# Attention scores laid out by query half, two plain groups of heads where there were four, and a normalisation whose rows go through memory

## The chip, the cores and the metric

The kernel runs on one core of a Trainium2 chip. The metric is the device time of one execution in microseconds (us). Three runs of the kernel before took 2332.04, 2332.18 and 2333.17 us, so its time is the median, 2332.18 us. The engines are called PE (matmuls; PEld loads its weights), DVE (vector work), ACT (scalar work, copies and casts), POOL (here mostly the issue of stores) and SP (the issue of loads).

## The reference

One step of a four-layer decoder over 1024 prompt tokens and 8 single-token samples, width 2048, all in float32. Layers "A" mix by pooling, layers "B" by attention within a window of 128 over keys and values that are projected once. The kernel computes one layer of each kind:

```
A:  z = x @ w_in_a                 # 2048 -> 4096: a branch u and a gate
    y = (group_linear(pool(u) - u) * scale * silu(gate)) @ w_out_a
    h = layer_norm(ALPHA * x + y)
kv: k, v = h @ w_kv                # 4 heads of 64, k rotated
B:  z = h @ w_in_b                 # 2048 -> 4096: 32 query heads of 64, and a gate
    s = q . k / 8 within the window of 128, else -1e30
    m = max(max_k s, sink)         # a learned sink for each head
    p = exp(s - m) / (sum_k exp(s - m) + exp(sink - m))
    y = ((p @ v) * silu(gate)) @ w_out_b
    out = layer_norm(ALPHA * h + y)
```

Outputs are the rows of both paths and the new states of pool, keys and values.

## The kernel before

**Products.** A float32 product is made of three matmuls in a rounded float32 type: high parts with high, high with low, low with high. So every 128x1024 tile of weights that arrives is first cast by ACT (L488, the high part), then DVE subtracts the cast from the tile (L503, the low part, here called the prep). A weight tile then feeds 24 matmuls; that is called a run here, and runs are numbered from the program's start.

**Two ways to multiply.** Tokens are cut into chunk 0 (512 prompt tokens) and chunk 1 (512 and the 8 samples). Most phases multiply by a Strassen-Winograd scheme (the method `seven`, L658 to L660): a pair of weight rows (four blocks) takes seven runs of 24 matmuls over half the tokens (256 or 260 columns). It needs sums of weight blocks (DVE adds, L293 or L346) and sums of the activations, made by `t_ops` (DVE, L826 to L829) and stored by POOL (L830) to the tiles tx, tg, th, to. Two phases are plain (the method `unit`, L686 to L688): four weight tiles per pair, 48 matmuls of 512 columns for each 128 rows of output. The phases run in the order ai (A's input product), ao (its output product), bi (B's input product with the attention in it), bo, each for both chunks; `PHASES` lists them, `PLAIN` names the plain ones. In bi the unit of work is a group p of 0 to 7: a pair of w_in_b for queries and one for gates, four heads of attention.

**Attention.** For each pair of heads (t, two per group) `attend` has the PE write scores into a bank S of PSUM (L1761), ACT copy one part of them into a memory tile (L1778), DVE put the other part in where the mask says so (`copy_predicated`, L1782, 128x1024 elements) and reduce to maxima (L1787); ACT takes the exponentials (L1798) and scales them (L1820), PE transposes (L1825), ACT copies out (L1833), DVE masks a part (L1834), PE multiplies with the values (L1863), DVE gates (L1891) and POOL stores the result (L1894, tile o).

**Order and memory.** ACT, DVE and PE each execute their instructions in the order in which the program issues them; nothing overtakes. Before each run `begin` loads weights for up to 7 runs ahead, casts up to 4 and preps up to 3 ahead (5, 4, 3 where plain). After each run `end` emits due events and, every so many runs (`every`) and if enough tiles are free (`room`), one step of a side job, such as the layer norm `ln_gen`. All of it lives in 54 tiles of on-chip memory (128x1040 floats, named m0 to m53; a trace shows them as m). A new tile is put where a tile was freed longest ago; one freed behind a store counts as freed 10 releases later (`Mem.full`, `Slot.free`). Before anything is written into such a place, its last reader, a store too, must be done.

**The norm between the layers.** `ln_gen` for chunk 1 runs as a side job in the plain bi phase: it subtracts the mean (L962), squares (L965), multiplies by the reciprocal deviation (L1000), scales and shifts (L991), stores h and calls `t_ops` for th1. The eight tiles stay on chip from the subtraction to the end.

Of the kernel before, what the change touches and what calls it, by code (L numbers as in the profile page):

```python
# [11 lines left out]
U8 = mybir.dt.uint8  # L12
# [4 lines left out]
P = 128  # L17
# [7 lines left out]
NH = 32  # L25
# [4 lines left out]
NEG = -1e30  # L30
TP = 512
NB = TP // P
# [18 lines left out]
    ("ai", 0, (0, 1)), ("ai", 0, (1, 4)), ("ai", 1, (0, 4)), ("ao", 0, None), ("ao", 1, None), ("bi", 0, (0, 4)),  # L51
    ("bi", 0, (4, 8)), ("bi", 1, (0, 8)), ("bo", 0, None), ("bo", 1, None),
# [129 lines left out]
class Kern:  # L182
    def __init__(self, ctx, tc, io):
# [12 lines left out]
        self.mki = one.tile([P, 2, P], U8, name="mki")  # L196
# [37 lines left out]
    def use_four(self, wide):  # L234
# [97 lines left out]
    def first_pair(self, name, q):  # L332
# [8 lines left out]
        def add(out, x, y, i):  # L341
            def go():
# [4 lines left out]
                self.nc.gpsimd.dma_start(ws[:, i, :], s[out].a[:, :1024])  # L347
# [3 lines left out]
        def free(*ks):  # L351
            return [lambda k=k: s.pop(k).free(k != "c") for k in ks]
# [20 lines left out]
    def build_stream(self):  # L373
        io = self.io
        w = []
        for kind, c, part in PHASES:
# [535 lines left out]
    def ln_gen(self, c, pre, acc, gc, bc, out, td):  # L912
# [39 lines left out]
        w = self.mem.full()  # L952
        q, v = w.a[:, :T], w.a[:, TMAX : TMAX + T]
        if c == 0:
            nc.vector.tensor_mul(q, mu, mu)
        else:
            sq, sqs = self.mem.full(), {}
            for p in range(10):
# [4 lines left out]
                if 1 <= p <= 8:  # L963
                    sqs[p - 1] = sq if p == 1 else self.mem.full()
                    nc.scalar.activation(flat(sqs[p - 1]), flat(pre[p - 1]), AF.Square)  # L965
                yield
# [5 lines left out]
            for go in self.j_steps(T, s2[:, 0], s2[:, 1], var, sq):  # L972
                go()
                yield
# [1404 lines left out]
```

## Time and profile before

| | us |
|---|---|
| median of three runs | 2332.18 |
| the profiled execution | 2332.49 |
| its span (first to last instruction) | 2330.7 |
| PE busy in the span | 2293.2 (98%) |
| DVE busy | 1908.7 (82%) |
| ACT busy | 1350.4 (58%) |
| POOL busy | 205.7 (9%) |

A row of the profile gives the line, the engine, the operation, the tile written and the tiles read, the shapes and the number of instructions (x); then, by view, the busy time, the mean duration in ns, the idle time before the group and what released it ("<-"). In a timeline the first two numbers are start and duration in us, and square brackets hold an idle time before the instruction. The line numbers in rows of before are those of the listing above; the changed kernel's lines lie a little further down (the prep is L503 in both, the t_ops L827 to L831, the predicated copy L1808).

### The profile page before, as it was taken

What the parts mean: (1) busy time and instruction counts of PE and PEld (TensorE: products, weight loads), DVE (VectorE), ACT (ScalarE), POOL (GpSimd) and SP (SyncE); (2) the same over time, 40 slices, a digit from 0 to 9 for tenths busy, and PEclk for the clock granted to TensorE, in tenths of its full rate; (3) what the DMA queues carried; (4) which work ended last, traced back from release to release, by engine and by line L of the source; (5) the groups of instructions that cost most, each with busy time, mean ns of one, the idle gap of its engine ahead of it and who ended that gap; (6) DMA issues with size and microseconds to landing.
All of it is one profiled execution on the core that took longest, in us unless ns stands there. A gap on an engine that the chain in (4) does not pass through costs nothing. (4 is left out here: it accounts for less than half of the span.)

```text
span 2330.7 us, 49775 instructions
## 1 busy us (share of the span) xinstructions
PE 2293.2 (98%) x19960; PEld 2199.7 (94%) x19960; DVE 1908.7 (82%) x2422; ACT 1350.4 (58%) x2492; POOL 205.7 (9%) x411
## 2 busy tenths in 40 slices
PE   8999999999999999999999999999999999999997
PEld 6899999999999999999788799999999999999997
DVE  8787998777878878988996888897676777889887
ACT  4444445544546546655465566785776678646556
POOL 0111110010000000000111111100000000000001
PEclk9999999999999999999999999999999999999999
DMA  8668789988899989999886666798777778799785
GB/s 293 221 228 312 267 293 356 330 302 297 278 325 320 340 280 325 323 385 345 274 333 240 241 220 236 240 321 288 246 245 221 221 229 307 243 361 379 250 303 198
DMA packets 250919, 665.04 MB, mean 285 GB/s; under 512 B 25760, under 2 KB 106432, under 8 KB 250688
## 3 DMA queue, kind: packets, MB, share of 16 engines
q1 hardware_dynamic: 205216, 496.79, 63.5%
q0 software_dynamic: 45472, 165.07, 18.4%
q8 instruction: 156, 2.56, 0.4%
q14 instruction: 75, 0.61, 0.1%
HBM read 466.66 MB, written 185.59 MB: 280 GB/s over the span
## 5 line engine op out<-in xcount | busy, mean ns | idle before, releaser
L658 PE MATMUL pD<-m,m 128*128 128x260 f32 (+1 forms) x4752 | 1346.2, 283 | 5.5 <-DVE m L619 3.9
L660 PE MATMUL pD<-m,m 128*128 128x260 f32 (+1 forms) x4752 | 1339.1, 282 | 3.3 <-DVE m L503 3.1
L659 PE MATMUL pD<-m,m 128*128 128x260 f32 (+1 forms) x4752 | 1339.3, 282 | 0.0
L658 PEld LDWEIGHTS pD<-m,m 128*128 128x128 f32 x4752 | 895.3, 188 | 10.9 <-issue 3.2
L660 PEld LDWEIGHTS pD<-m,m 128*128 128x128 f32 x4752 | 895.8, 189 | 4.0 <-DVE m L503 3.9
L659 PEld LDWEIGHTS pD<-m,m 128*128 128x128 f32 x4752 | 895.6, 188 | 0.5
L503 DVE TENSOR_TENSOR m<-m,m 128x1024 fp32r<-128x1024 f32 x674 | 814.6, 1220 | 72.7 <-ACT m L488 48.3
L488 ACT CAST m<-m 128x1024 fp32r<-128x1024 f32 x674 | 701.5, 1048 | 253.1 <-DVE m L346 77.7
L686 PE MATMUL pD<-m,m 128*128 128x512 f32 x448 | 179.7, 401 | 8.0 <-ACT m L769 8.0
L687 PE MATMUL pD<-m,m 128*128 128x512 f32 x448 | 177.6, 396 | 0.7 <-DVE m L778 0.7
L688 PE MATMUL pD<-m,m 128*128 128x512 f32 x448 | 177.2, 396 | 0.0
L778 DVE TENSOR_TENSOR m<-m,m 128x1024 fp32r<-128x1024 f32 (+1 forms) x120 | 147.1, 1229 | 9.5 <-ACT m L769 7.9
L631 ACT COPY m<-pD 128x260 f32<-128x260 f32 (+1 forms) x83 | 31.0, 374 | 189.8 <-PE pD L660 189.7
L769 ACT CAST m<-m 128x1024 fp32r<-128x1024 f32 (+1 forms) x120 | 125.8, 1051 | 10.3 <-DVE m L503 4.1
L346 DVE TENSOR_TENSOR m<-m,m 128x1024 f32<-128x1024 f32 x88 | 107.6, 1223 | 6.9 <-DMA m<-in_wia 4.2
L686 PEld LDWEIGHTS pD<-m,m 128*128 128x128 f32 x448 | 85.0, 190 | 27.9 <-ACT m L769 8.0
L687 PEld LDWEIGHTS pD<-m,m 128*128 128x128 f32 x448 | 85.0, 190 | 20.6 <-DVE m L778 1.9
L688 PEld LDWEIGHTS pD<-m,m 128*128 128x128 f32 x448 | 84.8, 189 | 19.8
L619 DVE TENSOR_TENSOR m<-pD,m 128x260 f32<-128x260 f32 (+1 forms) x86 | 36.5, 425 | 80.9 <-PE pD L660 80.8
L1798 ACT ACTIVATE m<-m,sm 128x128 f32<-128x128 f32 x256 | 99.2, 390 | 0.0
L1820 ACT ACTIVATE m<-m,sm 128x128 f32<-128x128 f32 (+1 forms) x320 | 93.9, 372 | 8.9 <-DVE sm L1806 5.5
L1088 PE MATMUL pD<-m,m 128*128 128x260 f32 (+1 forms) x528 | 91.2, 323 | 0.0
(249 smaller groups left out, 2157.2 us busy)
## 6 DMA issues: line engine op xcount, KB each, us to landing
m<-in_wia SPq DMA_DIRECT2D x124, 512.0 KB
m<-in_wib SPq DMA_DIRECT2D x120, 512.0 KB
swia<-m POOLq DMA_DIRECT2D x64, 512.0 KB, 5.0
m<-swia SPq DMA_DIRECT2D x64, 512.0 KB
m<-swoa SPq DMA_DIRECT2D x64, 512.0 KB
swib<-m POOLq DMA_DIRECT2D x64, 512.0 KB, 5.8
m<-swib SPq DMA_DIRECT2D x64, 512.0 KB
m<-swob SPq DMA_DIRECT2D x56, 512.0 KB
```

Of the source, the lines that this page charges most:

```text
L346: self.nc.vector.tensor_add(s[out].a[:, :1024], s[x].a[:, :1024], s[y].a[:, :1024])
L488: self.nc.scalar.copy(hi.r[:, :1024], self.stream[self.cast].src().a[:, :1024])
L503: self.nc.vector.tensor_sub(lo.r[:, :1024], s.src().a[:, :1024], hi.a[:, :1024])
L658: nc.tensor.matmul(ps[:, :TH], wh[:, s], h, start=new and k == 0, stop=False, skip_group_check=on)
L659: nc.tensor.matmul(ps[:, :TH], wh[:, s], l, start=False, stop=False, skip_group_check=on)
L660: nc.tensor.matmul(ps[:, :TH], wl[:, s], h, start=False, stop=k == 7, skip_group_check=on)
L686: nc.tensor.matmul(ps[:], wh[:, s], h, start=par == 0 and k == 0, stop=False)
L687: nc.tensor.matmul(ps[:], wh[:, s], l, start=False, stop=False)
L688: nc.tensor.matmul(ps[:], wl[:, s], h, start=False, stop=par == 1 and k == 7)
L769: self.nc.scalar.copy(h.r[:, :n], s.a[:, :n])
L778: self.nc.vector.tensor_sub(l.r[:, :n], s.a[:, :n], h.a[:, :n])
L1798: nc.scalar.activation(x["s3"][:, i, :], x["s3"][:, i, :], AF.Exp, bias=nm[:, i : i + 1], scale=0.125, accum_out=rs[:, i : i + 1],)
```

## The change

Four things are changed together.

1. The plain bi phase of chunk 0 takes groups 0 and 1 only; groups 2 to 7 are multiplied by the Strassen scheme. The plain pairs no longer form or store sums of weight blocks. Chunk 1 forms the sums of groups 0 and 1 itself and does not store them.
2. The bank S of scores is divided by query half u rather than by head j; what the mask governs is then 512 columns in place of 1024. ACT copies the rest; in chunk 0 it makes one more small copy. The zero fills of S at the start of the attention are gone.
3. The norm of chunk 1 stores seven of its eight tiles after the squares (POOL), and its third pass loads them again. That pass waits for run 56 after the plain phase's start, and so lies in the Strassen part of bi, at a step every 2.4 runs, with two free tiles asked for. Per tile it multiplies (L1010), scales and shifts (L1001), and makes t_ops with their store (L827 to L831).
4. `begin` loads 5 runs ahead, and up to 7 only while more than two tiles are free. Prep and cast go one run less ahead where at most one tile is free.

```diff
 PHASES = (
-    ("ai", 0, (0, 1)), ("ai", 0, (1, 4)), ("ai", 1, (0, 4)), ("ao", 0, None), ("ao", 1, None), ("bi", 0, (0, 4)),
-    ("bi", 0, (4, 8)), ("bi", 1, (0, 8)), ("bo", 0, None), ("bo", 1, None),
+    ("ai", 0, (0, 1)), ("ai", 0, (1, 4)), ("ai", 1, (0, 4)), ("ao", 0, None), ("ao", 1, None), ("bi", 0, (0, 2)),
+    ("bi", 0, (2, 8)), ("bi", 1, (0, 8)), ("bo", 0, None), ("bo", 1, None),
...
             self.S = self.pool4.tile([P, 2, 1024], F32, name=self.nm("pS"))
-            S4 = self.S[:].rearrange("p j (b k) -> p j b k", b=NB)
-            for j in range(2):
-                a, b = (slice(0, 64), slice(64, P))[:: 1 - 2 * j]
-                self.nc.vector.memset(S4[a, j, :, :64], 0.0)
-                self.nc.vector.memset(S4[b, j, :, 192:], 0.0)
...
-    def first_pair(self, name, q):
+    def first_pair(self, name, q, keep=True):
...
                 self.nc.vector.tensor_add(s[out].a[:, :1024], s[x].a[:, :1024], s[y].a[:, :1024])
-                self.nc.gpsimd.dma_start(ws[:, i, :], s[out].a[:, :1024])
+                if keep:
+                    self.nc.gpsimd.dma_start(ws[:, i, :], s[out].a[:, :1024])
 
             return go
 
         def free(*ks):
-            return [lambda k=k: s.pop(k).free(k != "c") for k in ks]
+            return [lambda k=k: s.pop(k).free(keep and k != "c") for k in ks]
...
-                if seven:
-                    for p in range(*part):
-                        w += pr("wib", p) + pr("wib", 8 + p)
-                else:
-                    for p in range(*part):
-                        q, g = pr("wib", p), pr("wib", 8 + p)
+                for p in range(*part):
+                    if not seven:
+                        q, g = ([self.lone(a) for a in self.quads("wib", n)] for n in (p, 8 + p))
                         w += q[:2] + g[:2] + q[2:] + g[2:]
+                        continue
+                    for n in (p, 8 + p):
+                        if c and p < PLAIN[1][2][1]:
+                            f = self.first_pair("wib", n, False)
+                            w += [f[i] for i in ORDER7]
+                        else:
+                            w += pr("wib", n)
...
     def begin(self):
         self.flush()
         a, b, d = self.ahead if self.strassen else (5, 4, 3)
-        if getattr(self, "ph", "") == "bi1" and len(self.mem.whole()) < 3:
-            a, b, d = min(a, 6), min(b, 3), min(d, 2)
-        self.load_to(self.e + a)
-        self.prep_to(self.e + d)
-        self.cast_to(self.e + b)
-        self.make_to(self.e + b + (1 if self.strassen else 0))
+        free = lambda: len(self.mem.whole())
+        self.load_to(self.e + min(a, 5))
+        while self.loaded < min(self.e + a, len(self.stream)) and free() > 2:
+            self.load_to(self.loaded + 1)
+        self.prep_to(self.e + (d if free() > 1 else d - 1))
+        self.cast_to(self.e + (b if free() > 1 else b - 1))
+        self.make_to(self.e + (b if free() > 0 else b - 1) + (1 if self.strassen else 0))
         self.e += 1
...
                     nc.scalar.activation(flat(sqs[p - 1]), flat(pre[p - 1]), AF.Square)
+                    if p < 8:
+                        nc.gpsimd.dma_start(away(p - 1), self.pair_view(pre[p - 1], T))
+                        pre.pop(p - 1).free(True)
...
+        if c:
+            while self.i < self.mark:
+                yield
+            load(6)
...
+        if c:
+            turns = (6, 7, 0, 1, 2, 3, 4, 5)
+            for n, p in enumerate(turns):
+                if n < 7:
+                    load(turns[n + 1])
+                t = self.pair_view(pre[p], T)
+                nc.vector.tensor_mul(t, t, b2(rr))
+                yield
+                affine(p)
+                yield
+                self.t_ops(t[:, 0], t[:, 1], td, p, T // 2)
+                pre[p].free(True)
+                yield
+        for p in range(10 if c == 0 else 0):
             load(p + 2)
             if p < 8:
                 t = self.pair_view(pre[p], T)
-                if c == 0:
-                    nc.vector.tensor_sub(t, t, b2(mu))
+                nc.vector.tensor_sub(t, t, b2(mu))
...
         def score():
             s, q, lastq = self.qs.pop((c, t))
             for b in range(NB):
-                for u in (0, 64):
+                for u in range(2):
                     for j in range(2):
                         r = slice(64 * j, 64 * j + 64)
-                        z = u if j == 0 else 64 - u
-                        o = self.S[z : z + 64, j, b * 256 + 64 - u : b * 256 + 256 - u]
-                        k = self.kT[t // 8][r, b * P + u : b * P + u + 192]
+                        z = 64 * (j ^ u)
+                        at = 256 * b + 64 * u
+                        o = self.S[z : z + 64, u, at : at + 192]
+                        k = self.kT[t // 8][r, b * P + 64 * u : b * P + 64 * u + 192]
+                        k = k.rearrange("p (m k) -> p m k", m=3)
                         nc.tensor.matmul(
-                            o.rearrange("p (m k) -> p m k", m=3), q[r, b * P + u : b * P + u + 64],
-                            k.rearrange("p (m k) -> p m k", m=3)[:, ::-1, :], start=True, stop=True,
+                            o.rearrange("p (m k) -> p m k", m=3), q[r, b * P + 64 * u : b * P + 64 * u + 64],
+                            k if u else k[:, ::-1, :], start=True, stop=True,
...
             b0 = 0
             if c == 0:
-                nc.gpsimd.memset(s3[:, 0:2, :], NEG)
+                nc.gpsimd.memset(sc[:, :192], NEG)
+                nc.scalar.copy(sc[:, 192:256], p4[:, 0, 1, 64:])
                 b0 = 1
-            nc.scalar.copy(s4[:, b0:], p4[:, b0:, :, P : 2 * P])
+            nc.scalar.copy(s4[:, b0:], p4[:, b0:])
...
             nc.vector.copy_predicated(
-                s4, self.mki[:, None, :, :].to_broadcast([P, NB, 2, P]), p4[:, :, :, 0:P]
+                x["sc"][:, :1024].rearrange("p (b v k) -> p b v k", b=NB, v=4)[:, :, 1:3, :],
+                self.mki[:, None, None, :].to_broadcast([P, NB, 2, 64]),
+                bass.AP(tensor=a.tensor, offset=a.offset, ap=[a.ap[0], (256, NB), (1216, 2), (1, 64)]),
...
-                x["wp"].a[:, :512].rearrange("p (b i k) -> p b i k", b=NB, i=2), mixed(slice(0, NB)),
+                x["wp"].a[:, :512].rearrange("p (b i k) -> p b i k", b=NB, i=2),
+                PT.rearrange("p (b i k) -> p b i k", b=NB, i=4)[:, :, 0:2, :],
...
+                                p = x["w"].a[r, :1024].rearrange("p (i q) -> p i q", q=64)
+                                i, e = (4 * b - 2 * k) % 16 + j, 4 * b + 3 - 2 * k - j
+                                if e > i:
+                                    p = p[:, i : e + 1 : e - i, :]
+                                else:
+                                    p = p[:, e : i + 1 : i - e, :][:, ::-1, :]
...
             elif (kind, c) == ("bi", 0) and not self.strassen:
+                self.mark = self.i + 56
...
+            elif (kind, c) == ("bi", 0):
+                self.every, self.room = 2.4, 2
...
-    k = (i + 64) % P
-    return cst, np.stack([k[None, :] <= q[:, None] for q in (i, k)], axis=1).astype(np.uint8)
+    return cst, (h[None, :] <= i[:, None] % 64).astype(np.uint8)```

How the rows stand on DVE, first: the t_ops for one tile of th1 (m with a number is a memory tile, then come counts of uses and names) and the prep that comes behind them. Before, this lay in the plain phase; POOL stores the t_ops' tile, m48:

```order
L826 TENSOR_TENSOR m48_1640_13922<-m24_1555_13007 128x260
L827 TENSOR_TENSOR m48_1640_13922<-m24_1555_13007 128x260
L828 TENSOR_TENSOR m48_1640_13922<-m24_1555_13007,m48_1640_13922 128x260 [waits DVE_49]
L829 TENSOR_TENSOR m48_1640_13922<-m24_1555_13007,m48_1640_13922 128x260 [waits DVE_49]
L503 TENSOR_TENSOR m44_1642_13930<-m13_1631_13762,m39_1638_13829 128x1024 [waits DMAHW6_49,DMASW7_49]
L293 TENSOR_TENSOR m13_1631_13762<-m36_1626_13708,m13_1631_13762 128x1024 [waits DVE_49]
```

The change, at run 391, in the Strassen part of bi for chunk 0, behind the mask and the maxima of a pair of heads:

```order
L1808 COPY_PREDICATED m42_1777_15336<-mki_77,pS_212_12834 128x4x128 [waits Activation_49,Pool_49]
L1815 TENSOR_REDUCE sm_267_15373<-m42_1777_15336 128x8 [waits DVE_49]
L1818 SCALAR_TENSOR_TENSOR sm_268_15374<-sm_267_15373,prm_75 128x8 [waits DVE_49]
L1819 TENSOR_TENSOR sm_269_15375<-sm_268_15374,prm_75 128x8 [waits DVE_49]
L827 TENSOR_TENSOR m35_1780_15379<-m32_1737_14832 128x260
L828 TENSOR_TENSOR m35_1780_15379<-m32_1737_14832 128x260
L829 TENSOR_TENSOR m35_1780_15379<-m32_1737_14832,m35_1780_15379 128x260 [waits DVE_49]
L830 TENSOR_TENSOR m35_1780_15379<-m32_1737_14832,m35_1780_15379 128x260 [waits DVE_49]
L503 TENSOR_TENSOR m35_1783_15390<-m12_1759_15086,m29_1779_15346 128x1024 [waits DMASW7_49,DVE_49,Activation_49]
L503 TENSOR_TENSOR m22_1786_15428<-m14_1774_15302,m32_1784_15392 128x1024 [waits DMAHW0_49,PE_49,Activation_49]
```

The prep now writes tile m35, the one that the t_ops just filled and whose store was issued an instant earlier (DMASW7 is that store's queue); before, it wrote m44, another tile than the t_ops' m48. The same stands at runs 406 (m12) and 420 (m1).

On ACT, at run 399 of the change, a cast stands behind the store of another t_ops (tile m32) in the same way:

```order
L1826 ACTIVATE m35_1803_15674,sm_275_15717<-m35_1803_15674,sm_276_15718 128x128
L600 ACTIVATE pD_279_15771<-pD_278_15730 128x256 [waits PE_49,Activation_49]
L488 CAST m32_1814_15777<-m20_1788_15464 128x1024 [waits DMASW6_49,DVE_49]
L1826 ACTIVATE m35_1803_15674,sm_275_15717<-m35_1803_15674,sm_276_15718 128x128 x4
L606 COPY m50_1787_15462<-pD_280_15781 128x256 [waits PE_49]
L609 COPY m50_1787_15462<-pD_279_15771 128x256 [waits PE_49]
L488 CAST m11_1818_15853<-m36_1798_15636 128x1024 [waits DVE_49]
```

The cast waits for the store (DMASW6) of m32, which POOL issued in the same run; behind it on ACT stand four exponentials and two evictions of PSUM. Run 413 has the same with m10.

More of the change, by code (lines that the diff above doesn't have):

```diff
@@ L195, in __init__ @@
         self.cst = one.tile([P, N_CST], F32, name="cst")
-        self.mki = one.tile([P, 2, P], U8, name="mki")
+        self.mki = one.tile([P, 64], U8, name="mki")
         self.jr = one.tile([P, P], F32R, name="jr")
@@ L974, in ln_gen @@
                 yield
+            w = self.mem.full()
+            q, v = w.a[:, :T], w.a[:, TMAX : TMAX + T]
         yield from self.quiet()
@@ L992, in affine @@
             nc.sync.dma_start(out[:, 2 * p : 2 * p + 2, :], t)
-        for p in range(10):
+        if c:
[12 more added lines that the diff above has]
+        for p in range(10 if c == 0 else 0):
             load(p + 2)
@@ L2293, in _consts @@
         cst[:, o : o + w - 1] = w / (np.arange(w - 1) + 1.0)
-    k = (i + 64) % P
-    return cst, np.stack([k[None, :] <= q[:, None] for q in (i, k)], axis=1).astype(np.uint8)
+    return cst, (h[None, :] <= i[:, None] % 64).astype(np.uint8)
 def kernel(**inputs):
@@ L2338 @@
     sinks = x["sinks_b"][0]
-    prm[:, C_SINK : C_SINK + NH] = sinks[None, _HEADS]
+    two = sinks[_HEADS].reshape(1, 16, 2)
+    prm[:64, C_SINK : C_SINK + NH] = two.reshape(1, NH)
+    prm[64:, C_SINK : C_SINK + NH] = two[:, :, ::-1].reshape(1, NH)
     prm[:, C_SDEC : C_SDEC + 2] = np.tile(sinks.reshape(2, 2, 1, 8), (1, 1, NDEC, 1)).reshape(2, P).T
```

20 lines of the change are left out of this document (8 added, 12 removed).

## The prediction

> **What bounds the kernel now.** I began with the page's busy shares and the waits of PE.
>
> ```profile
> span 2330.7 us, 49775 instructions
> PE 2293.2 (98%) x19960; PEld 2199.7 (94%) x19960; DVE 1908.7 (82%) x2422; ACT 1350.4 (58%) x2492; POOL 205.7 (9%) x411
> ...
> PE pD L686 <- ACT m L769: 8.0, 1, 8.0
> PE pD L658 <- DVE m L619: 3.9, 4, 1.3
> PE pD L660 <- DVE m L503: 3.1, 2, 2.6
> PE pD L1466 <- DVE m L1456: 1.9, 1, 1.9
> PE pO L1863 <- ACT m L1833: 1.8, 1, 1.8
> ```
>
> PE is busy for 98% of the span, and its largest wait is the 8.0 us of the start. So the time is PE's work, and an edit counts if it changes that work or makes PE stand. The phase that the change rebuilds, bi of chunk 0, lies from about 1087 to 1525 us; a table of windows shows plain bi, Strassen bi, and bi of chunk 1:
>
> ```profile
> core 0: us, PE busy (x) PEld busy (x) DVE busy (x) ACT busy (x) POOL busy (x), PEclk, DMA share, GB/s
> 1087.00:1341.00 254.00, 251.29 (x1650) 205.12 (x1650) 211.16 (x278) 138.29 (x311) 38.51 (x78) 0.99 0.77 276
> 1341.00:1525.00 184.00, 182.12 (x2048) 178.23 (x2047) 161.78 (x197) 129.05 (x307) 24.03 (x54) 1.00 0.72 240
> 1525.00:2018.00 493.00, 490.83 (x5437) 481.30 (x5436) 376.64 (x518) 352.13 (x826) 28.47 (x62) 1.00 0.78 255
> ```
>
> PE is busy for 99% there too, but DVE is close behind in the Strassen part (161.78 of 184 us, 88%). A DVE that loses some us there cannot make them up quickly. In this the danger lies.
>
> **PE's own work.** Per group, plain is 4 pair halves of 48 matmuls, 192 of 512 columns; Strassen is 2 pairs of 7 runs of 24, 336 of 256 columns. The intervals of issue, from the timeline of PE and from a window with Strassen work alone:
>
> ```profile
> 1299.80 0.39 PE L686 MATMUL pD<-m,m 128*128 128x512 f32 x1
> ...
> 1303.03 0.39 PE L688 MATMUL pD<-m,m 128*128 128x512 f32 x1
> ...
> 830.00:880.00 50.00, 50.00 (x425) 50.00 (x425) 32.61 (x33) 22.87 (x31) 1.09 (x2) 1.00 0.81 264
> ...
> 1373.44 0.29 PE L658 MATMUL pD<-m,m 128*128 128x256 f32 x1
> ...
> 1376.22 0.28 PE L660 MATMUL pD<-m,m 128*128 128x256 f32 x1
> ```
>
> The 512-column rows lie 14 intervals apart: 3.23/14 = 0.2307 us, 44.3 us per group. The window gives 50.00/425 = 0.1176 us, 39.5 us per group; the run in bi (24 rows, 23 intervals) 0.1209 us, 40.6 us. A group gains 3.7 to 4.8 us; two groups **7.4 to 9.5 us**, of which I take 8.5.
>
> **Scores.** The predicated copy over 512 columns will cost about what the masking product costs, which also reads 512 columns of PSUM:
>
> ```profile
> L503 DVE TENSOR_TENSOR m<-m,m 128x1024 fp32r<-128x1024 f32 x674 | 814.6, 1220 | 72.7 <-ACT m L488 48.3 <-ACT m L965 5.0 <-issue 4.8
> L1782 DVE COPY_PREDICATED m<-mki,pS 128x1024 f32<-128x1024 uint8 x32 | 42.2, 1319 | 0.0
> L1787 DVE TENSOR_REDUCE sm<-m 128x8 f32<-128x1024 f32 x32 | 39.1, 1221 | 1.1
> L1834 DVE TENSOR_TENSOR m<-pS,cst 128x512 f32<-128x512 f32 x32 | 22.1, 692 | 66.3 <-ACT m L1833 66.3
> L826 DVE TENSOR_TENSOR m<-m 128x260 f32<-128x260 f32 x32 | 13.5, 422 | 1.7 <-DMA m<-o 0.8 <-PE pD L659 0.8
> ```
>
> DVE gets 32 × (1.32 − 0.69) = 20 us back and pays 14.6 of them for the preps of the two new Strassen groups (12 more tiles at 1.22). Neither is on PE's path: the 2293 us of PE cover them. Without that cover the net of 5.4 us would be a gain. The memsets and stores left out, the small ACT copy and the norm's 14 extra transfers (the DMA share is 0.72 to 0.77) cost nothing by themselves for the same reason.
>
> **The stall at 1324 us.** Before, ACT's timeline shows a cast that waited for DVE's sums, and the copy that PE needs behind it; then PE's gap, and the clock:
>
> ```profile
> 1322.06 1.05 ACT L488 CAST m<-m 128x1024 fp32r<-128x1024 f32 x1 [3.06 <-DVE m L346]
> ...
> 1323.12 0.39 ACT L1798 ACTIVATE m<-m,sm 128x128 f32<-128x128 f32 x1
> ...
> 1325.60 1.00 ACT L1833 COPY m<-pS 128x1024 f32<-128x1024 f32 x1
> ...
> 1326.65 0.33 PE L1863 MATMUL pO<-m,m 64*64 64x128 f32 x2 [1.82 <-ACT m L1833]
> ...
> 1327.38 0.37 PE L1863 MATMUL pO<-m,m 64*64 64x64 f32 x2 [0.28 <-DVE m L1834]
> ...
> 354.00:357.80 3.80, 1.24 (x11) 1.04 (x10) 3.70 (x7) 1.45 (x2) 0.00 (x0) 1.00 1.00 382
> 357.80:361.40 3.60, 3.60 (x20) 3.60 (x19) 3.60 (x5) 3.57 (x7) 0.00 (x0) 0.53 1.06 379
> 1327.20:1330.80 3.60, 3.42 (x30) 2.83 (x31) 3.60 (x5) 0.95 (x6) 0.64 (x2) 0.53 1.05 388
> 2034.60:2038.20 3.60, 3.60 (x33) 3.60 (x32) 3.57 (x5) 0.48 (x1) 0.69 (x2) 1.00 1.04 311
> ```
>
> After a gap of 2.6 us (at 354) and one of 1.82 us the clock was granted at 0.53 for 3.6 us, which costs 3.6 × 0.47 = **1.7 us**; after a gap of 1.33 us (at 2033) it was not. The sums of plain pairs that held DVE there fall away, so the stall goes: −1.8 − 0.3 (a second, short gap) − 1.7 = **−3.8**; it may come back at the new border of plain and Strassen, so 0 is the other bound.
>
> The Trainium skill, "TensorE: Matmul & The Clock Gate", section "HAM oscillation — how this bites in real kernels", has PE throttled for idle gaps over about 3.4 us. By that rule gaps of 2 to 3 us would cost no clock, and the sum below would be 5.1 lower, 2337.8. The trace disagrees: 1.82 us was followed by 0.53.
>
> **The waits that the change adds.** In the Strassen part of bi the places in memory run out, since the norm's tiles and their t_ops come on top. A load, cast or prep then goes to whatever was freed last, and at five runs that is the tile of the t_ops whose store has just been issued: preps on DVE at 391, 406 and 420, casts on ACT at 399 and 413. Before, the shortest distance in Strassen bi was two to three runs. How long such a store takes, from the views of the tiles th and o:
>
> ```profile
> L830 POOL DMA_DIRECT2D th<-m x16: 531/531/542, 977.7 to 1222.0; - x16
> ...
> DMA to landing us min/median/max: 2.9/6.8/9.1
> ...
> L1894 POOL DMA_DIRECT2D o<-m x32: 539/547/565, 1211.5 to 2018.0; - x32
> ...
>   ACT m L605: 5.9, 1
>   ACT m L1820: 3.4, 1
> ...
> DMA to landing us min/median/max: 2.3/4.8/7.9
> ```
>
> So 4.8 to 6.8 us (2.3 to 9.1 at the ends) from the issue to the landing. A run is 24 × 0.1176 = 2.8 us.
>
> *Preps.* At 391 DVE has, from the end of run 390: a prep 1.22, the predicated copy 0.69, the reduction 1.22, four t_ops 1.69, so the store leaves at 4.8 and lands at 9.6 to 11.6. The prep ends 1.22 later, at 10.8 to 12.8. PE needs it three runs on, at 8.5: PE stands for 2.3 to 4.3 us. At 406 and 420 the t_ops themselves wait for the end of the run whose weights lay in their tile: 1.69 + 4.8 to 6.8 + 1.22 = 7.7 to 9.7 against two runs, 5.6: 2.1 to 4.1. I take **3.2 each, 9.6**, and the half clock behind each, **5.1**. Bounds: with 2.9 us to landing nearly 0; with 9.1, 6.5 each and 24.6 with the clock.
>
> *Casts.* The nearest row is an eviction of ACT that waited 5.90 us for a store of o; PE's gap behind it was 1.33 us:
>
> ```profile
> 2023.75 0.37 ACT L605 COPY m<-pD 128x256 f32<-128x256 f32 x1 [5.90 <-DMA o<-m]
> ...
> 2034.25 0.36 PE L658 MATMUL pD<-m,m 128*128 128x256 f32 x1 [1.33 <-DVE m L619]
> ```
>
> Here four exponentials and two evictions stand behind the waiting cast, and three PSUM banks take turns, so PE lacks a bank after three runs, 8.5 us; the evictions come at 9.5 to 11.5 (1.69 + 4.8 to 6.8 + the cast 1.05 + four exponentials 1.6 + 0.37). That is 1 to 3 us: I take 2.5 with part of a half clock, **5 for both**; bounds 2 × 1.33 = 2.7 and 2 × 4.7 = 9.4.
>
> *The rest.* Five more preps and casts follow such a store by one run; a run less to wait leaves 0 to 1 us each: **2** (0 to 5). In chunk 1 the sums of groups 0 and 1 are formed by DVE, 16 adds × 1.22 = 20 us over 56 runs with their preps; by the order's rows at these durations DVE's work in the first 14 runs is 1.06 of PE's time: **1** (0 to 3).
>
> **The sum**, against the profiled span: 2330.7 − 8.5 − 3.8 + 9.6 + 5.1 + 5 + 2 + 1 = 2341.1. Around the span lie 1.8 us (2332.49 − 2330.7), which gives **2342.9**. The profiled execution is 0.3 us over the median, which changes nothing.
>
> **Rivals.**
> *A, the waits are covered.* If stores land as at the low end (2.3 to 2.9 us), or DVE runs ahead further than I have it, PE keeps its gain: 2330.7 − 8.5 − 3.8 + 0 to 4 + 1.8 = **2320 to 2324**, faster. For it: the waits of 3.4 and 5.9 us for stores of o together cost PE 1.33. Against it: those stood on ACT, which has slack; the new ones stand on DVE, at 88% and more. It decides from landings under about 3.5 us.
> *B, gain and waits cancel.* At 4.5 us to landing the preps cost 1.9 each with one half clock, 7.4, the casts 2.7: 2318.4 + 7.4 + 2.7 + 3 + 1.8 = **2333**.
> *C, halves of scores one after the other.* Both heads' matmuls, in different row tiles of PE, now write one bank at a time, where each had its own. If they took turns, the burst would double at worst:
>
> ```profile
> L1761 PE MATMUL pS<-m,m 64*64 64x192 f32 x1024 | 47.9, 325 | 1.4 <-DVE m L1729 1.4
> ```
>
> that is +47.9 on A's figure, about **2370**. The Trainium skill, "TensorEngine Tiling (Array Packing)", section "Restrictions and Gotchas", says that different row tiles cannot access the same PSUM bank at the same time. No run here shows it; the two write different halves of the partitions, so I give it little.
>
> **How the numbers follow.** Forecast 0.47, A 0.30, B 0.18, C 0.03, other mishaps 0.02. The range, 2318 to 2353, holds A, B and the forecast up to landings near 9 us; the forecast's own range is 2335 to 2353. Within 0.2% of 2332.2 (what a measurement tells from no change) is 2327.5 to 2336.8: all of B and a bit of A's upper end and the forecast's lower. Faster 0.31, same 0.18, slower 0.51.
>
> **What would show it.** In the changed profile: PE waits for L503 of 2 to 4 us near runs 391, 406 and 420, with the prep idle behind the DMA of th1, and windows at 0.53 behind them; ACT casts that wait about 5 us for th1 at 399 and 413; no wait for L1858's copy at the border; the predicated copy near 0.7 us; the score's burst unchanged. If the th1 stores land in under 3.5 us or PE shows no gap there, A is right. If the gaps are there and the time still falls, the gain of PE's work was sized too small.

## The result: 2.2% slower

The changed kernel takes 2384.03 us (median of five runs, 2382.89 to 2384.76) against 2332.46 us before (five runs beside it). The ratio is 1.0221, with a 95% interval of 1.021 to 1.0232: 51.6 us slower. The forecast was slower, 2342.9 us, with 2353 as the upper end; the size is far outside.

The page's head and the waits of PE, in the order of their sums (engine, tile, line, what it waited for: us in total, times, longest):

```profile
span 2380.4 us, 50358 instructions
PE 2307.0 (97%) x20248; PEld 2227.4 (94%) x20248; DVE 1906.2 (80%) x2430; ACT 1366.6 (57%) x2530; POOL 199.2 (8%) x402
```
```profile
PE pD L661 <- DVE m L503: 13.8, 11, 3.9
PE pD L659 <- ACT pD L600: 11.6, 3, 5.9
PE pD L1892 <- ACT m L615: 8.7, 4, 3.5
PE pD L687 <- ACT m L770: 8.1, 1, 8.1
PE pS L1785 <- DVE m L1751: 5.6, 2, 4.0
PE pD L659 <- DVE m L620: 5.4, 5, 2.5
PE pS L1705 <- ACT m L2086: 5.4, 1, 5.4
```

The start's 8.1 us stayed. All else at the top is new or larger: preps (L503) 3.1 before, 13.8 now; evictions of PSUM (L600) 1.1 before, 11.6 now; and L1892, L1785 and L1705, whose like had at most 1.8 us before. Over all its rows this view has 28.0 us before and 64.7 now, +36.7.

The other part is the clock. Two rows of a table of windows, behind the gap of 5.33 us that ends at 1381, show it (the clock is the third number from the end):

```profile
1381.00:1384.60 3.60, 3.52 (x16) 3.52 (x17) 0.63 (x1) 1.40 (x5) 0.53 (x1) 0.50 1.04 295
1384.60:1388.00 3.40, 3.40 (x28) 3.40 (x27) 2.10 (x4) 2.81 (x10) 0.00 (x0) 0.86 0.91 323
```

A low clock costs only while PE works. With windows of 3.6 us over the whole span, the sum of PE's busy time × (1 − granted clock) is 2.8 us before and 22.1 now, +19.3. PE stands for 2330.7 − 2293.2 = 37.5 us before and for 2380.4 − 2307.0 = 73.4 now, +35.9. The span grew by 49.7, so 49.7 − 35.9 − 19.3 = −5.5 is left for PE's own work. The loss is PE standing and the half clock that follows; the work saved by part 1 makes up for little of it, and comes out smaller than the 8.5 of the forecast.

Where it stands, in the timelines of DVE, PE, POOL and ACT (start, duration, and in brackets the idle time before):

```profile
1318.36 1.23 DVE L503 TENSOR_TENSOR m<-m,m 128x1024 fp32r<-128x1024 f32 x1 [4.04 <-DMA th<-m]
...
1349.25 2.36 DVE L503 TENSOR_TENSOR m<-m,m 128x1024 fp32r<-128x1024 f32 x2 [6.14 <-DMA th<-m]
...
1350.53 0.39 PE L661 MATMUL pD<-m,m 128*128 128x256 f32 x1 [3.86 <-DVE m L503]
...
1371.16 0.53 POOL L831 DMA_DIRECT2D to<-m  x1 [0.86 <-DVE m L625]
...
1378.07 1.04 ACT L488 CAST m<-m 128x1024 fp32r<-128x1024 f32 x1 [7.42 <-DMA to<-m]
1383.23 1.05 ACT L488 CAST m<-m 128x1024 fp32r<-128x1024 f32 x1 [2.20 <-DMA th<-m]
...
1381.08 0.58 PE L659 MATMUL pD<-m,m 128*128 128x256 f32 x1 [5.33 <-ACT pD L600]
...
1395.13 0.37 ACT L615 COPY m<-pD 128x256 f32<-128x256 f32 x1 [2.93 <-DVE m L1751]
1395.56 0.33 PE L1892 MATMUL pD<-m,m 64*64 64x128 f32 x2 [2.40 <-ACT m L615]
```

The second row is the prep for run 394, which the forecast named, with PE's gap of 3.86 us behind it (3.2 was forecast). The first row, the prep for run 388, is one of those that follow a store by a run. The cast at 1378 waits for a store of *to*, not of th1: ACT has been at it since 1370.65 (1378.07 − 7.42), before that store left. Only the next cast, at 1383, waits for th1. Four exponentials and two evictions stand behind that one, as behind the cast that the program issues at run 399, for run 403; so the cast at 1378 is the one before it, for run 402. The last two rows are a third kind: ACT's eviction waits for a tile that DVE's rotation of q (L1751) has just let go of.

Another stand is outside Strassen bi. DVE waited 10.14 us, up to 1118, for the copies that swap k's halves on chip (0.73 before), and PE's 5.39 us at L1705, which end at 1135, follow. The windows of these 14 us, before and then now (the last but one column is the DMA share):

```profile
1104.90:1111.00 6.10, 6.10 (x28) 4.97 (x27) 1.09 (x2) 4.28 (x5) 0.00 (x0) 1.00 0.98 270
1111.00:1118.50 7.50, 7.50 (x34) 6.04 (x34) 6.70 (x8) 1.64 (x2) 0.55 (x1) 1.00 0.79 266
```
```profile
1104.90:1111.00 6.10, 6.10 (x28) 4.96 (x27) 2.45 (x2) 3.92 (x4) 0.53 (x1) 1.00 1.05 413
1111.00:1118.50 7.50, 7.50 (x34) 6.04 (x34) 0.00 (x1) 1.53 (x2) 0.00 (x0) 1.00 1.03 312
```
```profile
1113.35 2.36 DVE L1622 TENSOR_TENSOR m<-m,m 128x1024 f32<-128x1024 f32 x2 [0.73 <-DMA m<-m]
```
```profile
1118.50 2.36 DVE L1644 TENSOR_TENSOR m<-m,m 128x1024 f32<-128x1024 f32 x2 [10.14 <-DMA m<-m]
```

The DMA share is 1.05 and 1.03 where it was 0.98 and 0.79, and 413 and 312 GB/s are moved where it was 270 and 266. Five of the norm's stores of its tiles (p, 520 KB each) leave from 1089.7 to 1104.4 us, just ahead.

### The profile page after: what moved, and what is told of

Its sections match the earlier page's. It is cut to its first block, busy times and chain, and to the rows that moved or that the text cites. A ratio compares the mean times of both kernels' runs of the same rounds, so it can differ in the third digit from the quotient of the medians.

```text
span 2380.4 us, 50358 instructions
## 1 busy us (share of the span) xinstructions
PE 2307.0 (97%) x20248; PEld 2227.4 (94%) x20248; DVE 1906.2 (80%) x2430; ACT 1366.6 (57%) x2530; POOL 199.2 (8%) x402
## 3 DMA queue, kind: packets, MB, share of 16 engines
q8 instruction: 158, 2.59, 0.4%
## 5 line engine op out<-in xcount | busy, mean ns | idle before, releaser
L659 PE MATMUL pD<-m,m 128*128 128x260 f32 (+1 forms) x4976 | 1415.8, 285 | 17.5 <-ACT pD L600 11.6
L661 PE MATMUL pD<-m,m 128*128 128x260 f32 (+1 forms) x4976 | 1408.0, 283 | 14.0 <-DVE m L503 13.8
L660 PE MATMUL pD<-m,m 128*128 128x260 f32 (+1 forms) x4976 | 1407.5, 283 | 0.0
L659 PEld LDWEIGHTS pD<-m,m 128*128 128x128 f32 x4976 | 942.1, 189 | 23.9 <-ACT pD L600 12.5
L661 PEld LDWEIGHTS pD<-m,m 128*128 128x128 f32 x4976 | 942.9, 189 | 16.4 <-DVE m L503 16.4
L503 DVE TENSOR_TENSOR m<-m,m 128x1024 fp32r<-128x1024 f32 x686 | 828.7, 1219 | 102.7 <-ACT m L488 56.4
L488 ACT CAST m<-m 128x1024 fp32r<-128x1024 f32 x686 | 714.2, 1048 | 296.3 <-DVE m L341 92.4
L341 DVE TENSOR_TENSOR m<-m,m 128x1024 f32<-128x1024 f32 x120 | 146.7, 1222 | 8.2 <-DMA m<-in_wia 5.1
L632 ACT COPY m<-pD 128x260 f32<-128x260 f32 (+1 forms) x87 | 32.5, 373 | 191.5 <-PE pD L661 191.4
L687 PE MATMUL pD<-m,m 128*128 128x512 f32 x320 | 128.7, 402 | 8.1 <-ACT m L770 8.1
L770 ACT CAST m<-m 128x1024 fp32r<-128x1024 f32 (+1 forms) x120 | 125.7, 1052 | 14.4 <-DVE m L503 4.4
L688 PE MATMUL pD<-m,m 128*128 128x512 f32 x320 | 127.4, 398 | 0.7 <-DVE m L779 0.7
L689 PE MATMUL pD<-m,m 128*128 128x512 f32 x320 | 127.3, 398 | 0.4 <-DVE m L503 0.4
L620 DVE TENSOR_TENSOR m<-pD,m 128x260 f32<-128x260 f32 (+1 forms) x90 | 38.1, 424 | 78.1 <-PE pD L661 78.1
L1826 ACT ACTIVATE m<-m,sm 128x128 f32<-128x128 f32 x256 | 99.2, 390 | 0.0
L1110 PE MATMUL pD<-m,m 128*128 128x260 f32 (+1 forms) x528 | 91.3, 323 | 0.0
L609 ACT COPY m<-pD 128x260 f32<-128x260 f32 (+1 forms) x90 | 33.6, 373 | 87.6 <-PE pD L661 87.2
L687 PEld LDWEIGHTS pD<-m,m 128*128 128x128 f32 x320 | 61.1, 191 | 22.4 <-ACT m L770 8.1
```

The costliest lines, as they stand in the source:

```text
L341: self.nc.vector.tensor_add(s[out].a[:, :1024], s[x].a[:, :1024], s[y].a[:, :1024])
L488: self.nc.scalar.copy(hi.r[:, :1024], self.stream[self.cast].src().a[:, :1024])
L503: self.nc.vector.tensor_sub(lo.r[:, :1024], s.src().a[:, :1024], hi.a[:, :1024])
L659: nc.tensor.matmul(ps[:, :TH], wh[:, s], h, start=new and k == 0, stop=False, skip_group_check=on)
L660: nc.tensor.matmul(ps[:, :TH], wh[:, s], l, start=False, stop=False, skip_group_check=on)
L661: nc.tensor.matmul(ps[:, :TH], wl[:, s], h, start=False, stop=k == 7, skip_group_check=on)
```

## The experiments

Theory W: the loss is waits in and around Strassen bi, above all for stores whose tile is reused at once. Rivals: C, the score matmuls take turns in a PSUM bank; N, the norm's way through memory costs wherever it lies; D, DVE and ACT are simply too full there; S: the seven stores behind the squares cause the stand near 1130 us, DVE's wait up to 1118 and PE's behind it. The kernel before was run again beside each group of kernels, with medians of 2331.96 to 2333.31 us; so a difference between kernels of different groups is good to 1 or 2 us.

### Part 2 alone, and the change without it

The first kernel is the kernel before with the hunks of the scores only; the second has all hunks but those.

> The kernel before with the new score layout alone (part 2). Theory W (the loss comes from DVE, ACT and transfers waiting in and around the Strassen part of bi, as parts 1, 3 and 4 bring it): DVE gets about 32 x (1.32 - 0.735) = 19 us back, off PE's path, so 2326 to 2333 us. Rival C (score matmuls of both row tiles take turns in a bank): the score bursts double, +30 to +48 us, about 2370.

> The change with the old score layout (parts 1, 3 and 4 without 2). Theory W: the loss stays, and DVE has 19 us more work where it is already behind: 2384 to 2400 us. Rival C: the loss goes, about 2335 us.

Measured: 2330.28 us against 2332.93 before (ratio 0.9989, interval 0.9979 to 0.9998), and 2382.56 us (1.0214, 1.0199 to 1.0229). The first kernel's groups of score matmuls and predicated copies:

```profile
L1758 PE MATMUL pS<-m,m 64*64 64x192 f32 x1024 | 47.8, 324 | 0.0
L1781 DVE COPY_PREDICATED m<-mki,pS 128x512 f32<-128x512 uint8 x32 | 23.5, 734 | 0.0
```

The scores take 47.8 us, 47.9 before: C has fallen. The copy takes 734 ns where 692 was taken, so DVE has 18.7 us less. That bought about 2.6 us; PE's gap at the border of plain and Strassen, 1.82 us before, is 1.26 there, and the half clock behind it did not come. In the change the new scores are worth nothing either way, within the intervals: the old scores' 19 us of DVE work do not show, and 2382.56 lies just under the range expected. Of all the kernels run, the scores alone are the only one whose interval lies below the kernel before, and only just (0.9998).

### Part 1 undone: four plain groups

```diff
-    ("ai", 0, (0, 1)), ("ai", 0, (1, 4)), ("ai", 1, (0, 4)), ("ao", 0, None), ("ao", 1, None), ("bi", 0, (0, 2)),
-    ("bi", 0, (2, 8)), ("bi", 1, (0, 8)), ("bo", 0, None), ("bo", 1, None),
+    ("ai", 0, (0, 1)), ("ai", 0, (1, 4)), ("ai", 1, (0, 4)), ("ao", 0, None), ("ao", 1, None), ("bi", 0, (0, 4)),
+    ("bi", 0, (4, 8)), ("bi", 1, (0, 8)), ("bo", 0, None), ("bo", 1, None),
```
(and the pairs store their sums again). A second kernel also starts the norm's third pass as soon as it can:
```diff
-                self.mark = self.i + 56
+                self.mark = self.i
```

> The change without part 1: four plain groups, so that the norm's third pass (from run 56 of the phase on) lies in the plain part, where a run lasts 5.6 us; the norm through memory, the new begin and the new scores stay. Theory W: the waits for stores of th1 in Strassen bi go (some 36 us with their half clocks), the stall near 1130 us stays (8 us), PE has its 8.5 us of work back: 2335 to 2345 us. Rival N (the norm's way through memory costs by itself, by its transfers, wherever it lies): over 2365 us.

> Four plain groups with everything else of the change, and the norm's third pass not held back to run 56, so that it is done in the plain part; no prep or cast is then put behind a store of the same run. Theory W: the loss of the variant with four plain groups (2392.8 us) was that its third pass still reached into Strassen bi; now 2335 to 2345 us, of which 8 are the stall near 1130 us. Rival N (the norm through memory, or the new begin, costs wherever it lies): over 2365 us.

Measured: 2392.76 us (ratio 1.0257, 1.0242 to 1.0273) and 2347.32 us (1.0064, 1.0049 to 1.0079). The first missed its expectation by nearly 50 us and seemed to speak for N. Its trace says otherwise: with the mark at run 56 and a step every few runs its third pass went on to 1535 us, through all of Strassen bi, and ACT waited there 4.7 to 9.6 us four times for stores of th1 and to. Started early, the same pass lies in the plain part, no cast or prep follows a store of th1 or to by less than two runs, and 45 us are gone. So N in its large form has fallen: it matters most where the pass lies. It is not all of it wrong, for 14 us over the kernel before remain, and the next experiment shows that part of them is the price of the norm's stores. What is left of the second kernel's loss is in two rows of PE's waits:

```profile
PE pO L1887 <- ACT m L1853: 7.7, 1, 7.7
PE pS L1700 <- ACT m L2081: 5.4, 1, 5.4
```

The second is the stand near 1130; the first, at the border of plain and Strassen, follows a DVE sum that waited 6.99 us for a load of weights (w_in_b). The expected 2335 to 2345 us had only the second.

### The stores behind the squares

```diff
-                        nc.gpsimd.dma_start(away(p - 1), self.pair_view(pre[p - 1], T))
                         pre.pop(p - 1).free(True)
```

> The change without the seven stores of the norm's tiles behind the squares; the third pass loads the rows as they were before the mean was taken off, so that the subtraction is left out of the result. All tiles and the order stay. Theory S (these stores fill the DMA engines near 1090 to 1120 us, the copy that the rotation of k needs lands 10 us late, and PE stands for 5.4 us and gets a half clock): 7 to 9 us less than the change, about 2376 us, PE's wait at L1705 back to 0.6 us, the DMA share of 1100 to 1111 us back under 1. Rival (the copy is late for another reason, the changed place of its tile or the loads of weights): 2384 us.

Measured: 2376.0 us (ratio 1.0183, 1.0166 to 1.02), 8.0 less than the change, as S expected. DVE's rotation of k waits 2.92 us in place of 10.14 and starts 8 us earlier, and PE's wait at L1705 is gone from the view:

```profile
1110.20 2.36 DVE L1643 TENSOR_TENSOR m<-m,m 128x1024 f32<-128x1024 f32 x2 [2.92 <-DMA m<-m]
```
```profile
1104.90:1111.00 6.10, 6.10 (x28) 4.96 (x27) 3.15 (x3) 2.84 (x3) 0.55 (x1) 1.00 1.04 298
```

Nothing else differs between this kernel and the change: what ACT, DVE and PE execute, the tiles and the loads are the same. One point of the expectation failed: the DMA share of 1104.9 to 1111 us stays at 1.04 (in the 4.9 us ahead of it, it fell from 1.04 to 0.92). What fell is the amount moved, 413 to 298 GB/s. A full share by itself does not say, then, that a copy will be late; that these stores made it late is shown by leaving them out.

### The stores of th1 and to

In the first kernel the store reads another tile when it is the norm's t_ops that are stored; in the second also when it is a store of to between the start of the norm's third pass and the end of Strassen bi. That tile, `away`, is the norm's tile of mean and deviation.

```diff
-        nc.gpsimd.dma_start(dst[:, kp], t)
+        src = t if self.away is None else self.away.v(4, TH)
+        nc.gpsimd.dma_start(dst[:, kp], src)
```

> The change with th1's eight stores reading another tile of the same size (the one that holds the norm's mean and deviation) and not the one that the t_ops filled, so th1 gets other values; every instruction, every tile and the order stay, but what is written into the t_ops' tiles next need not wait for a store. Theory W: the waits of preps 388, 394, 409, 423 and of the casts for 403 and 417 on th1 and with them 30 to 40 us go: 2344 to 2356 us. Rival D (DVE is simply too full in Strassen bi, the waits only shift where it shows): under 10 us less, over 2374 us.

> The change with the stores of th1 and of to that fall into the norm's third pass reading another tile (th1 and to get other values); instructions, tiles and order stay. With th1 alone the time was 2363.5, and the two casts behind stores of to were left, PE's gaps of 4.9 and 6.5 us with their half clocks and the gaps of 2.7 us behind them. Theory W (the casts wait for these stores and for nothing else): some 15 to 26 us less, 2337 to 2348 us. Rival D (DVE and ACT are too full there): 2358 to 2364 us.

Measured: 2363.45 us (ratio 1.0136, 1.0121 to 1.0151), 20.6 less than the change; and 2343.74 us (1.0048, 1.0033 to 1.0063), 40.3 less. What ACT, DVE and PE execute, and on which tiles, is the same in these kernels. Without these two kinds of stores behind the tiles **40 of the 51.6 us** are gone, half with th1 and half with to. D, as the main cause, has fallen.

One thing more differs, which the expectations did not foresee: a store that reads another tile no longer waits for the t_ops, and POOL issues it much earlier. The sixteen stores of th, of which the last eight are th1's, in the change and then in the second kernel (the last two numbers ahead of the semicolon are the first and the last start):

```profile
L831 POOL DMA_DIRECT2D th<-m x16: 531/532/542, 976.5 to 1503.3; - x16
```
```profile
L832 POOL DMA_DIRECT2D th<-m x16: 531/532/557, 977.2 to 1172.5; - x16
```

So the edit also takes the traffic of these stores out of Strassen bi, and by itself it can't tell a wait for the tile from a wait for a busy DMA queue. The waits of the change between 1270 and 1520 us can, in part; all transfers with over 1.2 us are shown:

```profile
DVE m L503 <- DMA th<-m: 16.5, 4, 6.1
DVE m L1644 <- DMA m<-m: 3.4, 1, 3.4
...
ACT m L488 <- DMA to<-m: 15.4, 2, 7.9
ACT m L488 <- DMA th<-m: 5.1, 2, 2.9
```

With the smaller ones DVE and ACT wait 38.2 us for stores of th and to, and 5.5 us for all other transfers; the second kernel has 2.0 us of the latter. So the traffic can account for a few us, and the tiles for the rest. The kernel under "A begin that leaves such tiles alone" tests it with the stores in place.

My expectation of 30 to 40 us for th1 alone was too high, since the casts for 402 and 416, behind stores of to, hold ACT up before those for 403 and 417 do. PE's waits of the second kernel:

```profile
PE pD L1895 <- ACT m L615: 7.5, 3, 2.6
...
PE pS L1708 <- ACT m L2089: 5.4, 1, 5.4
PE pD L661 <- DVE m L503: 5.2, 5, 2.6
...
PE pD L659 <- ACT pD L600: 1.9, 3, 0.9
```

Preps are down from 13.8 to 5.2 (2.6 of it at 354 us, as before), ACT's evictions L600 from 11.6 to 1.9. What stays is L615 and the stand near 1130.

### Both kinds taken away

The first of these leaves out the p stores and reads another tile for th1; the second does so for to as well.

> Both of the last two: th1's stores read another tile, and the seven stores behind the squares are left out (the subtraction missing from the result). If the two causes add: 2336 to 2348 us, and what is then left over the kernel before is DVE's load and the waits for stores of to and o. If theory S is wrong, the same as with the other tile alone.

> Both kinds of waits taken away at once: the stores of th1 and to read another tile, and the seven stores behind the squares are left out (the subtraction missing from the result). If the causes add up: 2343.7 - 6 to 8 = 2335 to 2338 us; the rest over the kernel before would be PE's gaps of 2.7 us at L1892 (ACT's eviction L615 into a tile that DVE's rotation has just let go) and those at the border, against 8.5 us of saved work. If they do not add: 2343 us.

Measured: 2357.23 us (ratio 1.0103, 1.0086 to 1.012), over its range, which had been reckoned with 30 to 40 us for th1; with the 20.6 measured, 2384.03 − 20.6 − 8.0 = 2355.4. And 2336.33 us (1.0013, 1.0003 to 1.0022). 8.0 and 40.3 would add to 48.3; the kernel is 47.7 under the change. The causes add, as far as the noise and the clock allow (PE's busy time × (1 − granted clock) is 10.0 us in this kernel's trace and 6.0 in the one without the waits for th1 and to). What is left over the kernel before is 1 to 5 us, by the interval, though PE's work is less (8.5 us by the forecast, some 6 by the traces): the three gaps at the line that is L1892 in the change remain, 7.5 us (L615 in the waits, the longest 2.6), each followed by a stretch of half clock.

### A begin that leaves such tiles alone

```diff
-        free = lambda: len(self.mem.whole())
+        free = lambda: sum(max(self.mem.f[i]) <= self.mem.clock for i in self.mem.whole())
```
The line stands twice, in `begin` and in `x_tick`, which makes the casts and preps of activations; both are altered, though the expectation speaks of one.

> The change with one line of begin altered: as free count only tiles that no fresh store still reads (those past the 10 releases). Preps and casts are then issued a run later where only such tiles are left, and only one is put within a run of a store. Theory W: most of the 36 us behind the stores goes and the shorter lead gives back a part: 2340 to 2358 us. Rival D (too little memory is the cause, and a prep that is issued later is late just the same): over 2372 us.

> The same, and the seven stores behind the squares are replaced by a second subtraction of the mean in the third pass (7 x 1.24 = 8.7 us more for DVE, 3.7 MB less to store). Theory S: the stall near 1130 us goes, 8 us less than the kernel without this, 0 to 3 us given back by DVE: 2333 to 2352 us.

Measured: 2362.91 us (ratio 1.0129, 1.0112 to 1.0146) and 2369.15 us (1.0156, 1.0141 to 1.0172). Both lie over their ranges, the first by 5, the second by 17 us. In the first kernel the stores of th1 stay in Strassen bi (1289 to 1488 us), and from 1270 to 1520 us DVE and ACT wait 5.8 us for stores of th and to where they waited 38.2, at most 2.2 at a time. So with these transfers in place, and the casts and preps kept off their tiles, 21.1 us are gone. The tiles cost more than that, it seems, since the shorter lead came back as many small gaps:

```profile
PE pD L659 <- ACT pD L600: 10.1, 9, 1.5
PE pS L1785 <- DVE m L1751: 8.6, 5, 2.2
```

So it seems that the tiles are too few for a prep issued three runs ahead, the norm's pass and the attention at once: part of what D claimed, in its memory form, is right. With the subtraction the time is 6 us longer, and PE's stand at L1705 only shrank to 2.8 us. That DVE's 8.7 us more fall where it has none to spare is my reading; no run shows it.

### Three plain groups, the norm on chip

```diff
-    ("ai", 0, (0, 1)), ("ai", 0, (1, 4)), ("ai", 1, (0, 4)), ("ao", 0, None), ("ao", 1, None), ("bi", 0, (0, 2)),
-    ("bi", 0, (2, 8)), ("bi", 1, (0, 8)), ("bo", 0, None), ("bo", 1, None),
+    ("ai", 0, (0, 1)), ("ai", 0, (1, 4)), ("ai", 1, (0, 4)), ("ao", 0, None), ("ao", 1, None), ("bi", 0, (0, 3)),
+    ("bi", 0, (3, 8)), ("bi", 1, (0, 8)), ("bo", 0, None), ("bo", 1, None),
```
(part 3 undone; with two plain groups and the norm on chip the 54 tiles do not suffice).

> Three plain groups (0 to 2), the norm of chunk 1 on chip and in the plain part as before (part 3 undone), the new scores, the new begin, pairs without sums. No prep or cast stands within a run of a store of th or to. Theory W: PE saves half of the 8.5 us, the scores' 2.6 us come on top, no stall near 1130 us: 2324 to 2331 us. Rival D (DVE too full, or memory too tight, as soon as a group moves to Strassen): over 2335 us.

Measured: 2330.96 us (ratio 0.9994, 0.9985 to 1.0003): no change that can be told from before. No wait of over 1 us for a store of th or to is left, but the work saved (4.2 us by the forecast's reckoning) is spent elsewhere. D's figure, over 2335, did not come. Beside the scores alone, its trace has gaps of 1.2 us (an eviction at the border, DVE's), 1.6 and 2.4 us (q's rotation, L1730):

```profile
PE pD L659 <- DVE m L620: 6.4, 6, 2.5
PE pD L661 <- DVE m L503: 4.3, 4, 2.0
PE pS L1764 <- DVE m L1730: 3.9, 2, 2.4
```

## Why the prediction was right in its kind and wrong in its size

- **PE's work, −8.5.** Right in direction, and probably too large. PE's busy time less the lost clock (as reckoned above) is 2289.1 to 2294.4 us in the four traces with four plain groups, 2281.5 to 2288.2 in the nine with two; the means differ by 6. The spread within each kind is as large, so this is rough.
- **Preps behind th1, 9.6 + 5.1.** The places were right: the preps for 394, 409 and 423 waited 6.14, 4.75 and 5.05 us (the second is put down to ACT's copy L609). So was the landing time: 3.1 / 5.1 / 7.1 us (min, median, max) for the eight stores of th1, where 4.8 to 6.8 was taken. The sizes were not: 394 left a gap of 3.86 us with a half clock behind it, but 409 and 423 left 0.7 and 1.8, and 1.0 and 0.7 us, with no half clock.
- **Casts behind th1, 5.** The casts for 403 and 417 waited 2.20 and 2.85 us, not about 5, and no gap of PE over 0.6 us stands behind them but L615's: ACT had come to them late, from the casts for 402 and 416.
- **19.7 for these two terms against 20.6 measured without th1's stores** is partly luck. The 20.6 also hold the prep for 388, which was in another term, and what the stores' traffic cost; of the places named, 394 alone cost what was forecast.
- **"Five more preps and casts follow such a store by one run ... 0 to 1 us each: 2".** This is the step that failed most. The five are the preps for 380, 388 and 431 and the casts for 402 and 416; they waited 1.20, 4.04, 1.25, 7.42 and 7.94 us. The two casts, behind stores of to, left PE's two longest gaps in Strassen bi, 5.33 and 5.89 us. Taking to's part away brought 19.7 us. The reasoning gave the engine a run's time between store and cast. But a distance in runs is a distance in the order of issue: ACT had nothing else to do, came to the cast before the store had left and waited it out in full. And then the next cast, behind th1, held it again, with the exponentials and evictions behind both.
- **"The norm's 14 extra transfers cost nothing by themselves".** Wrong: 8.0 us. I looked at the mean DMA share of the whole stage (0.77), which hid that the share between 1105 and 1111 us was 0.98 already, with a copy on DVE's and PE's path in the middle of it.
- **The stall at 1324 us, −3.8.** It went, as forecast: no wait for L1858's copy is left in the view. PE stands 3.48 us at nearly the same time, up to 1330, for another cause (L615, with the prep for 388 ahead of it).
- **Not in the sum at all:** L615 behind L1751, a tile given from DVE's rotation to ACT's eviction with no transfer between. I counted reuse behind stores only. In the kernel without store waits these three gaps are 7.5 us, before their half clocks. With the two failed terms put right the sum is 2342.9 + 17.7 + 8.0 = 2368.6. The 15 us that are still lacking may lie in these gaps and their half clocks, at q's rotation (L1785 behind L1751, 5.6 us) and in the smaller saving of PE's work; no run took them away one by one, so their shares stay open.
- **The half clock behind gaps of 2 to 3 us.** Gaps of 2.40 and 2.47 us (at 1395 and 1459) were followed by half clock, as the forecast took it and against the rule of 3.4 us that it quotes; but others of this length were not, as the last section shows.
- **Rival A** fell because the landings are 5.1 us at the median and not under 3.5. **B** took 4.5, which is near, and failed by the same two terms as the forecast. **C** fell by direct measurement.

The forecast took the one mechanism it had found in its clearest form, five places. The same mechanism at a distance of one run made another 20 us, and the stores that the norm sends among the copies 8.

## What to carry to other kernels

When a pool of tiles is nearly empty, the next tile handed out is the one freed last, even if the rule is to take the one freed longest ago, and every consumer of the pool is chained to the slowest reader just before it, a store's landing above all. Count such reuse at zero and one step's distance alike: an engine that is idle waits the store out in full, and an in-order engine makes all that is queued behind it wait too. When an experiment changes what a store reads, look in its trace when the store leaves: here it left up to 330 us earlier, and the experiment changed more than was meant. Read the DMA share in the microseconds around a transfer on the path, not over the stage, before calling further transfers free.

## What the runs showed of the hardware that was not expected

The half clock is not set by the length of a gap alone. Gaps in PE's timeline, of the change and then of the kernel with three plain groups, and after each the window behind them:

```profile
1291.41 0.39 PE L659 MATMUL pD<-m,m 128*128 128x256 f32 x1 [0.41 <-ACT pD L600]
1293.26 0.50 PE L661 MATMUL pD<-m,m 128*128 128x256 f32 x1 [1.35 <-DVE m L503]
...
1421.26 0.39 PE L661 MATMUL pD<-m,m 128*128 128x256 f32 x1 [1.84 <-DVE m L503]
```
```profile
1293.00:1296.60 3.60, 3.34 (x16) 3.34 (x17) 3.57 (x4) 2.09 (x8) 0.53 (x1) 0.55 0.72 272
...
1421.00:1424.60 3.60, 3.34 (x46) 3.20 (x50) 3.50 (x5) 2.88 (x10) 0.00 (x0) 1.00 0.27 105
```
```profile
1801.99 1.21 PE L1764 MATMUL pS<-m,m 64*64 64x192 f32 x24 [2.35 <-DVE m L1730]
```
```profile
1802.00:1805.60 3.60, 3.60 (x76) 3.46 (x77) 3.41 (x6) 1.50 (x2) 0.00 (x0) 1.00 0.55 173
```

Behind 0.41 and 1.35 us the clock was granted at 0.55; behind 1.84 and behind 2.35 us it was full. So a bound between 1.33 and 1.82 us, which the forecast's reading implies, does not hold. Plainer still are two kernels that have the same gap at the same place: the third gap of L615 in the one without the waits for th1 and to, and in the one that leaves out the stores behind the squares as well, each with the window behind it.

```profile
1431.71 0.33 PE L1895 MATMUL pD<-m,m 64*64 64x128 f32 x2 [2.58 <-ACT m L615]
...
1431.70:1435.30 3.60, 3.59 (x98) 3.52 (x99) 3.60 (x5) 2.84 (x7) 0.63 (x2) 1.00 0.13 51
```
```profile
1423.21 0.48 PE L1894 MATMUL pD<-m,m 64*64 64x128 f32 x2 [2.59 <-ACT m L615]
...
1423.20:1426.80 3.60, 3.59 (x61) 3.59 (x65) 3.60 (x5) 2.41 (x6) 0.63 (x2) 0.50 0.09 35
```

Behind 2.58 us the clock was full, behind 2.59 us it was granted at 0.50. The Trainium skill, "TensorE: Matmul & The Clock Gate", section "What's actually happening", has the clock judged over a free-running window of about 3.4 us. The place of a gap against such a window could tell these apart, but no run here shows where the windows lie. The longest gaps cost more than one such stretch: behind 5.33 us stand the two windows at 0.50 and 0.86 shown above.
